# A two-block network on one core: 92 instead of 84 expert chunks computed ahead, a new order of work in the mixers and in the state-space layer

## The chip, the cores and the metric

The kernel runs on one core of one Trainium2 chip. The metric is the device time of one execution in microseconds; before and after are compared by the median of several runs. The core's engines run side by side and each executes its own queue in order: PE (TensorE, matmuls; PEld is its weight load), DVE (VectorE), ACT (ScalarE), POOL (GpSimd) and SP (SyncE, which here only issues DMAs). An engine waits for another through semaphores.

## The reference, cut to what matters

One sequence of 512 tokens of width 1024 goes through two blocks. The first has two linear-attention mixers and a PEER layer (a mixture of 16384 tiny experts); the second has latent attention (MLA), a state-space layer (S5) and two MLPs.

```python
def mixer_output(t, states, n_chunks, hg_norm_g, gla_norm_g, w_br_hg, w_br_gla, w_o):
    o_hg = bidir(t["hg_q"], t["hg_k"], t["hg_v"], t["hg_lg"], states["hg"], n_chunks)       # 8 heads
    o_gla = bidir(t["gla_q"], t["gla_k"], t["gla_v"], t["gla_lg"], states["gla"], n_chunks) # 4 heads
    ...
def peer(h, wq, k1, k2, u, v):
    ...  # per token: 8 heads x top-16 of 16384 experts, and a softmax gate for each
        act = jax.nn.gelu(jnp.einsum("pd,ped->pe", xb, jnp.take(u, eb, axis=0)), approximate=False)
        return jnp.einsum("pe,ped->pd", (gb * act).astype(v.dtype), jnp.take(v, eb, axis=0))
    ...
def s5_mixer(...):
    ...
    _, _, xr, xi = lax.associative_scan(combine, (a_re_t, a_im_t, bu_re, bu_im), axis=1)
    y = (jnp.einsum('blgp,gcp->blgc', xr, c_re) - jnp.einsum('blgp,gcp->blgc', xi, c_im))
    y = y + d_skip * u32
    g = jax.nn.gelu(y)
    z = g * jax.nn.sigmoid(g @ w_glu + b_glu)
    return z @ w_out
```

`bidir` runs a chunkwise decayed attention forward and backward over each head and adds the two.

## The kernel before, in words

The order of each engine's queue comes from a scheduler that simulates the program as written, so the order of the Python calls, the number of buffers of each tile (`bufs`) and the simulated times decide it together. Each fp32 product is computed as three matmul passes over operands split in a high and a low half (`hi x whi`, `lo x whi`, `hi x wlo`); splitting a weight tile of 128 x 1024 costs one ACT cast (`whi`, L387) and one DVE subtraction (`wlo`, L388). A "block" below is one such product of eight 128-row pieces: 24 matmuls.

**Mixers (from 0 to about 1000 us).** First the eight HGRN heads, from about 585 to 856 us the four GLA heads. A GLA head (`gla`) projects values and keys, then the query `ps_q`, then the decays `ps_gk` of both directions (L1043: four short matmuls, whose result goes through ACT and DVE to `lg`), then two gates `ps_g` of 24 matmuls each. `direction` turns one direction's `lg` into a cumulated decay `b` on DVE, transposes the context keys on PE (`pt_c`, L840), multiplies `pkv_c` (L845), computes scores `sc` (L899) and updates states (`pt`, `pkv`).

**PEER (1000 to 2310 us).** 384 of the tokens ("dense", tiles of 384 columns) compute all 16384 experts, 128 at a time, with a matrix of gates that is zero where a token did not choose the expert; the other 128 tokens gather their 128 experts' rows of `u` and `v` by indirect DMA on POOL (`rows`) and multiply on DVE. A chunk `e` of 128 experts has a *hidden* block (`hidden`: weight tile `raw` of `u` from HBM, `pu` on PE, gelu on ACT to `hx` or `kx`), and an output block with the same chunk of `v`. Chunks come in 16 groups of 8. While DVE does the top-k selection (1000 to 1350 us) and then the spread (1350 to 1613 us), PE computes hidden blocks ahead: those of the list `AHEAD` are parked in a DRAM buffer (`he`, 192 KB each) and read back as `hx`; the 16 of `KEPT` (groups 0 and 1) stay in SBUF as `kx`. The spread builds the gate matrix: DVE compares with iota (`o`, L1365 to L1368), PE multiplies (`pg`, L1375), ACT copies (`gs`, L1377), SP writes two halves of a block of 32 tokens to DRAM (`gd`, L1379), 12 blocks. Then in the *weighted phase*, group by group, gates are read back (`gt`, L1095, 12 blocks of 128 columns at once, for 4 chunks), `kx` or `hx` is multiplied with them (L1106), split (`ahi`, `alo`), and eight output blocks (`ps`) add up over the group's chunks. `hx` has `HX` buffers, `gt` has `GT`. A group of which not all hidden chunks were done ahead computes the rest inside the phase: with 84 ahead, two blocks in each of the groups 2 to 15.

**Second block (2310 to 3529 us).** MLA, MLP, then S5 (2935 to about 3160 us), MLP. S5 works in 8 chunks of 128 channels: `project(c)` (`ps_u`, and a round trip of `u` through DRAM), `scan(c)` (`pw` from table `sT`, rotations from `rot` on DVE and POOL), `answer(c)` (`py` from tables `tt` and `cp`), `activate(c)` (a second round trip, gelu, split), then the gate product `ps_g`. The tables were made before and lie in DRAM; `S5In` loads them chunk by chunk, with two buffers for each kind of table.

Of the kernel before, what the change touches and what calls it, by code (L numbers as in the profile page):

```python
# [9 lines left out]
F32 = mybir.dt.float32  # L10
# [20 lines left out]
PI_IN = 3.1415925  # L31


AHEAD = [8 * g + i for i in range(8) for g in range(2, 16)][:84]
KEPT = range(16)

RING = 16
# [7 lines left out]
ADA_DVE = (2,)  # L45
ADA_M = [[2 * j, 2 * j + 1, 8 + 2 * j, 9 + 2 * j] for j in range(4)]
NGLU = 3
S5P = 5
HX = 5
GT = 3  # L50
PIN = True
GPIN = True
# [10 lines left out]
GBLK = TD // GTOK  # L63
# [275 lines left out]

class S5In:  # L340

    SHAPES = (("tt", [8, 128], 2), ("sT", [8, 128], 2), ("cp", [2, 512], 2), ("rot", [2, 2, 256], 2))

    def __init__(self, B, M):
        self.B, self.M, self.got = B, M, {}
# [22 lines left out]
class Build:  # L368
# [613 lines left out]
    def hgrn(self):  # L982
        nc, M, Q, ia = self.nc, self.M, self.Q, self.ia
        for hd in range(NH):
# [3 lines left out]
            keys, lgs = [], []  # L988
# [14 lines left out]
                keys.append(s)  # L1003
                lgs.append(lg)
            q = self.query(ia["w_hg"][hd, 2])
            runs = [self.direction(d, q, keys[d], lgs[d], 1.0, vt, 128, None) for d in range(2)]
            g = self.gate(ia["w_hg"][hd, 3])
            self.outputs(vt, 128, runs, [g], self.col("hgrn_norm_g"), hd)
            if hd == 0:

# [9 lines left out]
    def gla(self):  # L1020
# [7 lines left out]
        for hd in range(NG):  # L1028
# [3 lines left out]
            key = M.tile([128, T + TC], F32, tag="key", bufs=2, name="key")  # L1032
            nc.scalar.copy(out=key[:, 0:T], in_=ps[:])
            nc.scalar.copy(out=key[:, T:T + TC], in_=pc[:])
            q = self.query(ia["w_gq"][hd])
            lgs = []
            for d in range(2):
                bias = self.col("gk_b", d * 4 + hd)
                lg = M.tile([128, T + TC], F32, tag="lg", bufs=2, name="lg")
                parts = []  # L1040
                for t0, n in ((0, T), (T, TC)):
                    ps = self.G.tile([128, n], F32, tag="mm", bufs=3, name="ps_gk")
                    nc.tensor.matmul(ps[:], lhsT=gkw[d * 32:d * 32 + 16, hd * 128:hd * 128 + 128],  # L1043
                                     rhs=gr[d * 32:d * 32 + 16, t0:t0 + n], start=True, stop=True)
                    ex = self.A.tile([128, T], F32, tag="sg", bufs=2, name="ex")
                    nc.scalar.activation(out=ex[:, 0:n], in_=ps[:], func=AF.Abs, bias=bias)
                    parts.append((ex[:, 0:n], lg[:, t0:t0 + n]))
                    nc.vector.tensor_scalar(out=lg[:, t0:t0 + n], in0=ps[:], scalar1=bias, scalar2=0.0, op0=ALU.add,
                                            op1=ALU.min)
                for ex, _ in parts:  # L1050
                    nc.scalar.activation(out=ex, in_=ex, func=AF.Exp, scale=-1.0)
                for ex, to in parts:
                    nc.scalar.activation(out=ex, in_=ex, func=AF.Ln, bias=1.0)
                    nc.vector.tensor_tensor(out=to, in0=to, in1=ex, op=ALU.subtract)
                lgs.append(lg)
            runs = [self.direction(d, q, key, lgs[d], 1.0 / 16.0, vt, 256, None) for d in range(2)]
            gates = [self.gate(ia["w_gg"][2 * hd + i]) for i in range(2)]
            self.outputs(vt, 256, runs, gates, self.col("gla_norm_g", 0, 2), 2 * hd)


# [1 line left out]
    def peer(self):  # L1062
        tc, nc, ia, P = self.tc, self.nc, self.ia, self.P
        with tc.tile_pool(name="peer", bufs=1) as A, tc.tile_pool(name="peerd", bufs=1, space=DRAM) as DR, \
# [23 lines left out]
            with tc.tile_pool(name="pv", bufs=1) as M, tc.tile_pool(name="pvp", bufs=1, space=PSUM) as Q:  # L1088
                gates = {}

                def act(e):
                    g, n = e // 4, 4 * GTOK
                    if g not in gates:
                        gates[g] = M.tile([128, GBLK, n], F32, tag="gt", bufs=GT, name="gt")
                        nc.sync.dma_start(out=gates[g], in_=gd[:].rearrange("b p e t -> p b (e t)")[  # L1095
                            :, :, g * n:(g + 1) * n])
                    gt = gates[g][:, :, (e % 4) * GTOK:(e % 4 + 1) * GTOK]
                    x = kept.get(e)
                    if x is None:
# [722 lines left out]
    def s5_states(self, M, Q):  # L1822
# [89 lines left out]
        scan(0)  # L1912
        done = 0
        for c in range(8):
            if c + S5P < 8:
                project(c + S5P)
            if c < 7:
                scan(c + 1)
            answer(c)
            while done <= c and c + S5P >= 7:  # L1920
                activate(done)
# [43 lines left out]
```

## Time and profile before

| | us |
|---|---|
| runs | 3541.2, 3534.71, 3549.97 (median 3541.2) |
| profiled execution | 3531.33, its span 3529.1, mean granted TensorE clock 0.973 |
| mixers, 0 to 1000 | PE busy 957.53 of 1000 |
| selection and spread, 1000 to 1590 | PE busy 587.68 of 590, 237 GB/s |
| end of spread and weighted phase, 1590 to 2310 | PE busy 688.37 of 720, 308 GB/s |
| second block, 2310 to 3529 | PE busy 1155.39 of 1219, 129 GB/s |

Times in the table are stretches of the profiled execution; busy time is time in which the engine had an instruction running, and the rest is time that it stood idle. PE is idle for 140 us in all, and the clock granted to it is below full in some stretches. So time can come from three places: less work on PE, fewer waits, or a higher clock.

### The profile page before, as it was taken

To read this page: it belongs to the slowest core of one execution; us is meant where nothing else is said; L and a number is where in the kernel's file an instruction comes from. 1 tells how busy PE (TensorE), PEld (TensorE's weight loads), DVE (VectorE), ACT (ScalarE), POOL (GpSimd) and SP (SyncE) were. 2 spreads that over 40 slices of the span, in tenths; PEclk is the share of its full clock that TensorE was granted. 3 is DMA by queue.
4 is the path that set the end of the run, shared out by engine and by line. 5 is a ranking of instruction groups with operands and counts; after the bars stand their busy time and mean duration, and the time that the engine had idled before them with its cause. 6 is when DMAs were issued, how large, how long until landed. Compare 5 with 4: busy or idle time off the path is not lost.

```text
span 3529.1 us, 49456 instructions
## 1 busy us (share of the span) xinstructions
PE 3389.0 (96%) x18457; PEld 2981.8 (84%) x18457; DVE 2496.4 (71%) x4763; ACT 1573.9 (45%) x2480; POOL 620.0 (18%) x459
## 2 busy tenths in 40 slices
PE   8999999999999999996999999999999998899998
PEld 5888878787889999996999999976887778788887
DVE  5566676535657998987988988775897867773335
ACT  5576533545334335774333333344533344343333
POOL 3111100111100312333344444200000002300000
PEclk9999999999999999998999999999999998899999
DMA  5223365112624876889999999611367666523332
GB/s 199 90 84 97 96 209 189 48 37 87 184 72 122 286 243 235 335 298 304 335 319 338 334 339 335 215 57 41 115 209 219 202 188 179 144 79 94 96 96 66
DMA packets 280911, 636.52 MB, mean 180 GB/s; under 512 B 33440, under 2 KB 128800, under 8 KB 277216
## 3 DMA queue, kind: packets, MB, share of 16 engines
q1 hardware_dynamic: 233056, 490.75, 43.1%
q0 software_dynamic: 38144, 138.43, 10.7%
q10 hardware_dynamic: 9472, 4.20, 0.4%
q8 instruction: 145, 2.38, 0.3%
q14 instruction: 94, 0.77, 0.1%
HBM read 573.30 MB, written 64.18 MB: 181 GB/s over the span
## 4 chain that ended last, share of the span: by engine, by line
PE 71%; DVE 14%; DMA 6%; ACT 5%; issue 3%; SPq 1%; POOL 1%; DVEq 0%; ACTq 0%; POOLq 0%
PE ps L400 22%; PE pu L400 11%; PE ps_f L400 6%; PE ps_v L400 4%; PE ps L435 4%; PE ps_q L400 3%; DVE wlo L388 2%; PE pg L1375 2%; PE ps_l L400 2%; DMA modw<-in_modT_dram 2%; PE ps_g L400 2%; DVE modw L542 1%; PE pm L400 1%; PE pb L435 1%; DVE rows L1166 1%
## 5 line engine op out<-in xcount | busy, mean ns | idle before, releaser
L387 ACT CAST whi<-raw 128x1024 fp32r<-128x1024 f32 x547 | 572.1, 1049 | 967.9 <-PE ps L400 274.5
L388 DVE TENSOR_TENSOR wlo<-raw,whi 128x1024 fp32r<-128x1024 f32 x530 | 653.7, 1235 | 309.5 <-ACT whi L387 177.2
L400 PE MATMUL ps<-ahi,whi 128*128 128x384 f32 (+2 forms) x1560 | 330.7, 352 | 24.1 <-ACT ahi L517 19.4
L400 PE MATMUL ps<-alo,whi 128*128 128x384 f32 (+2 forms) x1560 | 334.0, 351 | 1.7 <-DVE alo L518 1.5
L400 PE MATMUL ps<-ahi,wlo 128*128 128x384 f32 (+2 forms) x1560 | 320.8, 347 | 0.0
L400 PEld LDWEIGHTS ps<-ahi,whi 128*128 128x128 f32 x1560 | 275.5, 191 | 50.2 <-ACT ahi L517 24.7
L400 PEld LDWEIGHTS ps<-alo,whi 128*128 128x128 f32 x1560 | 276.2, 189 | 23.0 <-DVE alo L518 3.3
L1145 POOL DMA_INDIRECT rows<-in_u_rows_dram,gidx x128 | 182.7, 1427 | 607.0 <-DVE gact L1166 406.6
L400 PEld LDWEIGHTS ps<-ahi,wlo 128*128 128x128 f32 x1560 | 272.3, 188 | 19.5 <-issue 0.2
L1145 POOL DMA_INDIRECT rows<-in_v_rows_dram,gidx x128 | 204.2, 1595 | 262.5 <-DVE gacc L1181 241.5
L400 PE MATMUL pu<-h_hi,whi 128*128 128x384 f32 x1024 | 203.7, 338 | 1.2 <-ACT hx L1077 1.2
L400 PE MATMUL pu<-h_hi,wlo 128*128 128x384 f32 x1024 | 202.5, 338 | 0.0
L400 PE MATMUL pu<-h_lo,whi 128*128 128x384 f32 x1024 | 201.0, 337 | 0.0
L400 PEld LDWEIGHTS pu<-h_hi,whi 128*128 128x128 f32 x1024 | 178.7, 188 | 2.1 <-ACT hx L1077 2.0
L400 PEld LDWEIGHTS pu<-h_lo,whi 128*128 128x128 f32 x1024 | 179.3, 188 | 0.0
L400 PEld LDWEIGHTS pu<-h_hi,wlo 128*128 128x128 f32 x1024 | 178.7, 188 | 0.1
L1181 DVE SCALAR_TENSOR_TENSOR gacc<-rows,ggate,gacc 128x1024 f32<-128x1024 f32 x127 | 162.4, 1279 | 0.1
L1166 DVE CUSTOM_DVE_ANT_0 rows<-rows,gx 128x1024 f32<-128x1024 f32 x128 | 154.4, 1221 | 2.7 <-DMA rows<-in_u_rows_dram,gidx 2.7
L1400 DVE SCALAR_TENSOR_TENSOR res<-ps,mod,res 128x512 f32<-128x512 f32 (+1 forms) x92 | 62.3, 679 | 113.1 <-PE ps L400 106.5
L388 POOL TENSOR_TENSOR wlo<-raw,whi 128x1024 fp32r<-128x1024 f32 x17 | 43.6, 2584 | 547.8 <-DVE wlo L388 406.2
L400 PE MATMUL ps_f<-h_hi,whi 128*128 128x512 f32 x464 | 119.8, 397 | 1.2 <-ACT whi L387 1.2
L517 ACT CAST ahi<-hx 128x384 fp32r<-128x384 f32 x112 | 56.4, 513 | 143.3 <-DVE hx L1106 143.3
(625 smaller groups left out, 7038.3 us busy)
## 6 DMA issues: line engine op xcount, KB each, us to landing
raw<-in_u_dram SPq DMA_DIRECT2D x128, 512.0 KB, 4.4
raw<-in_v_dram SPq DMA_DIRECT2D x128, 512.0 KB, 5.3
raw<-in_w_dram SPq DMA_DIRECT2D x128, 512.0 KB, 3.6
modw<-in_modT_dram SPq DMA_DIRECT2D x192, 256.0 KB, 4.1
gd<-gs SPq DMA_DIRECT2D x24, 1024.0 KB, 8.0
gt<-gd SPq DMA_DIRECT2D x32, 768.0 KB, 9.9
raw<-in_w_hg_dram SPq DMA_DIRECT2D x32, 512.0 KB, 3.6
res<-in_adaT_dram SPq DMA_DIRECT2D x64, 256.0 KB, 3.5
```

The costliest lines, as they stand in the source:

```text
L387: self.nc.scalar.copy(out=hi[:], in_=raw[:])
L388: (eng or self.nc.vector).tensor_tensor(out=lo[:], in0=raw[:], in1=hi[:].bitcast(F32), op=ALU.subtract)
L400: i = self.nc.tensor.matmul(ps, lhsT=w[a], rhs=x[b], start=start and n == 0, stop=stop and n == last)
L435: self.nc.tensor.matmul(ps[:, tok], lhsT=w[a][:, k], rhs=rhs(k, b, tok), start=(k == 0 and i == 0), stop=(k == 7 and i == 2))
L517: nc.scalar.copy(out=hi, in_=src)
L542: r = nc.vector.tensor_tensor_reduce(out=w[:], in0=w[:], in1=row[i][:], scale=1.0, scalar=start, op0=ALU.mult, op1=ALU.add, accum_out=out[ ...
L1145: self.nc.gpsimd.indirect_dma_start(out=t[:], out_offset=None, in_=self.ia[rows], in_offset=bass.IndirectOffsetOnAxis(ap=self.gidx[:, s:s ...
L1166: i = nc.vector.tensor_tensor_reduce(out=r[:], in0=r[:], in1=x[:], scale=1.0, scalar=0.0, op0=ALU.mult, op1=ALU.add, accum_out=act[:, s:s ...
L1181: i = nc.vector.scalar_tensor_tensor(out=acc[:], in0=r[:], scalar=w, in1=acc[:], op0=ALU.mult, op1=ALU.add)
L1375: nc.tensor.matmul(pg[:, j], lhsT=o2[:, q * 4 + j], rhs=o1[:, q * 4 + j], start=True, stop=True)
L1400: self.nc.vector.scalar_tensor_tensor(out=self.res[:, d, tok], in0=ps, scalar=self.gate1(n)[:, d:d + 1], in1=self.res[:, d, tok], op0=ALU. ...
```

## The change

Five edits. (1) `AHEAD` takes 92 chunks instead of 84: the seventh chunk of the groups 2 to 9 is computed before the weighted phase too. (2) `HX` goes from 5 to 4, and the gates of the first four chunks get a tile of their own in another pool, loaded in three pieces (the blocks 0 to 8, 9 to 10, and 11). (3) An HGRN head's gate is written between its two directions. (4) A GLA head's first decay is written ahead of the query, and gates and directions alternate. (5) In S5 three projections run ahead instead of five, a chunk's project call stands between the scan and the answer, and `tt` and `sT` have three buffers.

```diff
-AHEAD = [8 * g + i for i in range(8) for g in range(2, 16)][:84]
+AHEAD = [8 * g + i for i in range(8) for g in range(2, 16)][:92]
-S5P = 5
-HX = 5
+S5P = 3
+HX = 4
-    SHAPES = (("tt", [8, 128], 2), ("sT", [8, 128], 2), ("cp", [2, 512], 2), ("rot", [2, 2, 256], 2))
+    SHAPES = (("tt", [8, 128], 3), ("sT", [8, 128], 3), ("cp", [2, 512], 2), ("rot", [2, 2, 256], 2))
...
-            runs = [self.direction(d, q, keys[d], lgs[d], 1.0, vt, 128, None) for d in range(2)]
+            runs = [self.direction(0, q, keys[0], lgs[0], 1.0, vt, 128, None)]
             g = self.gate(ia["w_hg"][hd, 3])
+            runs.append(self.direction(1, q, keys[1], lgs[1], 1.0, vt, 128, None))
...
-            q = self.query(ia["w_gq"][hd])
-            lgs = []
-            for d in range(2):
+
+            def decay(d):
...
-                lgs.append(lg)
-            runs = [self.direction(d, q, key, lgs[d], 1.0 / 16.0, vt, 256, None) for d in range(2)]
-            gates = [self.gate(ia["w_gg"][2 * hd + i]) for i in range(2)]
+                return lg
+            lgs = [decay(0)]
+            q = self.query(ia["w_gq"][hd])
+            lgs.append(decay(1))
+            gates = [self.gate(ia["w_gg"][2 * hd])]
+            runs = [self.direction(0, q, key, lgs[0], 1.0 / 16.0, vt, 256, None)]
+            gates.append(self.gate(ia["w_gg"][2 * hd + 1]))
+            runs.append(self.direction(1, q, key, lgs[1], 1.0 / 16.0, vt, 256, None))
...
-                        gates[g] = M.tile([128, GBLK, n], F32, tag="gt", bufs=GT, name="gt")
-                        nc.sync.dma_start(out=gates[g], in_=gd[:].rearrange("b p e t -> p b (e t)")[
-                            :, :, g * n:(g + 1) * n])
+                        cuts = (0, GBLK - 3, GBLK - 1, GBLK) if g == 0 else (0, GBLK)
+                        gates[g] = (A if g == 0 else M).tile([128, GBLK, n], F32, tag=f"gt{min(g, 1)}",
+                                                             bufs=GT if g else 1, name="gt")
+                        for b0, b1 in zip(cuts, cuts[1:]):
+                            nc.sync.dma_start(out=gates[g][:, b0:b1], in_=gd[b0:b1].rearrange("b p e t -> p b (e t)")[
+                                :, :, g * n:(g + 1) * n])
...
         for c in range(8):
+            if c < 7:
+                scan(c + 1)
+
             if c + S5P < 8:
                 project(c + S5P)
-            if c < 7:
-                scan(c + 1)
             answer(c)
```

In the HGRN heads no engine's queue changes: the first row of PE that differs stands in the first GLA head. The three places below show what the scheduler makes of the rest. In each row stand the line, the operation, output and input tiles, the shape, and how often the row repeats; "before" is the first fence of each place.

**Place 1: PE at the third GLA head**, from the last projection to the first transposes. Before, the four `ps_gk` stand together behind `ps_q`:

```order
L400 MATMUL ps_q<-h_hi,whi 128x512 x8
L400 MATMUL ps_q<-h_lo,whi 128x512 x8
L400 MATMUL ps_q<-h_hi,wlo 128x512 x8
L1043 MATMUL ps_gk<-gr,gkw 128x512
L1043 MATMUL ps_gk<-gr,gkw 128x256
L1043 MATMUL ps_gk<-gr,gkw 128x512
L1043 MATMUL ps_gk<-gr,gkw 128x256
L400 MATMUL ps_g<-h_hi,whi 128x512 x8
L400 MATMUL ps_g<-h_lo,whi 128x512 x8
L400 MATMUL ps_g<-h_hi,wlo 128x512 x8
L400 MATMUL ps_g<-h_hi,whi 128x512 x5
L840 MATMUL pt_c<-ident,ck 128x128 x2
```

After, at the same place of the same engine:

```order
L1043 MATMUL ps_gk<-gr,gkw 128x512
L1043 MATMUL ps_gk<-gr,gkw 128x256
L400 MATMUL ps_q<-h_hi,whi 128x512 x8
L400 MATMUL ps_q<-h_lo,whi 128x512 x8
L400 MATMUL ps_q<-h_hi,wlo 128x512 x8
L1043 MATMUL ps_gk<-gr,gkw 128x512
L1043 MATMUL ps_gk<-gr,gkw 128x256
L400 MATMUL ps_g<-h_hi,whi 128x512 x8
L400 MATMUL ps_g<-h_lo,whi 128x512 x8
L400 MATMUL ps_g<-h_hi,wlo 128x512 x8
L840 MATMUL pt_c<-ident,ck 128x128 x2
```

The first two `ps_gk` moved ahead of the 24 `ps_q`, and the second gate moved behind the first direction's transposes, scores and states (not shown). In the first head `pt_c` stands directly behind the second pair of `ps_gk`, ahead of both gates.

**Place 2: SP at the end of the spread** (`gd` are the spread's writes, `gt` the gates read back, `raw` weight tiles of `u` and `v`). Before:

```order
L1379 DMA gd<-gs 128x2048 x2
L378 DMA raw<-in_v_dram 128x1024 x4
L1379 DMA gd<-gs 128x2048 x2
L378 DMA raw<-in_v_dram 128x1024 x2
L1379 DMA gd<-gs 128x2048 x4
L1095 DMA gt<-gd 128x12x128 x8
L378 DMA raw<-in_v_dram 128x1024 x8
```

After, the same engine from the ninth block's writes on:

```order
L1390 DMA gd<-gs 128x2048 x2
L1106 DMA gt<-gd 128x9x128
L378 DMA raw<-in_u_dram 128x1024 x4
L1390 DMA gd<-gs 128x2048 x2
L378 DMA raw<-in_u_dram 128x1024 x3
L1390 DMA gd<-gs 128x2048 x2
L378 DMA raw<-in_u_dram 128x1024
L1106 DMA gt<-gd 128x2x128
L378 DMA raw<-in_v_dram 128x1024 x3
L1390 DMA gd<-gs 128x2048 x2
L1106 DMA gt<-gd 128x128
L378 DMA raw<-in_v_dram 128x1024
```

Two of the three pieces of the first gates now stand ahead of the last write, three loads of `v` stand directly ahead of it, and eight loads of `u` came in. On PE the last six `pg` rows, which stood alone before, now have five hidden blocks (`pu`) between them, and three more blocks stand between the last `pg` and the first `ps`.

**Place 3: SP around the start of S5** (`tt`, `sT`, `rot`, `cp` are the tables of a chunk, `w_su` and `w_glu` weights, `decay` the last load ahead of the layer). Before:

```order
L378 DMA raw<-in_w_dram 128x1024 x2
L378 DMA raw<-in_w_su_dram 128x1024 x6
L1848 DMA decay<-d_dec 64x2x32 x2
L378 DMA raw<-in_w_su_dram 128x1024 x2
L378 DMA raw<-in_w_glu_dram 128x1024 x3
L359 DMA sT<-d_s 128x1024
L378 DMA raw<-in_w_glu_dram 128x1024
L359 DMA sT<-d_s 128x1024
```

After, from the same two weight loads on:

```order
L378 DMA raw<-in_w_dram 128x1024 x2
L378 DMA raw<-in_w_su_dram 128x1024
L359 DMA tt<-d_t 128x1024
L359 DMA sT<-d_s 128x1024
L378 DMA raw<-in_w_su_dram 128x1024 x5
L1859 DMA decay<-d_dec 64x2x32 x2
L378 DMA raw<-in_w_su_dram 128x1024 x2
L378 DMA raw<-in_w_glu_dram 128x1024 x3
L359 DMA sT<-d_s 128x1024 x2
```

The two big tables of the third chunk, 512 KB each, moved from behind the `w_glu` loads to ahead of `decay`; where one `sT` stood behind the first `w_glu` loads, two now stand together.

## Rows read from the trace of the kernel before

**Rows 1.** The page: the chain that ended last, shares by engine.

```profile
PE 71%; DVE 14%; DMA 6%; ACT 5%; issue 3%; SPq 1%; POOL 1%; DVEq 0%; ACTq 0%; POOLq 0%
```

**Rows 2.** Windows: length; busy PE, PEld, DVE, ACT, POOL; PE clock, DMA share, GB/s.

```profile
602.00:856.00 254.00, 241.46 (x1352) 198.09 (x1351) 118.85 (x228) 138.36 (x204) 30.54 (x32) 0.94 0.15 46
...
1590.00:1655.00 65.00, 37.48 (x191) 32.46 (x190) 44.01 (x70) 24.22 (x58) 16.91 (x13) 0.76 0.89 288
1660.00:1700.00 40.00, 39.74 (x225) 38.44 (x224) 39.38 (x63) 16.43 (x24) 18.94 (x15) 1.00 0.90 318
1708.00:2214.00 506.00, 503.34 (x2877) 501.10 (x2876) 447.87 (x568) 183.64 (x241) 216.01 (x138) 1.00 0.95 335
2900.00:2940.00 40.00, 32.79 (x238) 31.56 (x238) 33.37 (x90) 21.83 (x47) 1.95 (x4) 0.91 0.04 13
2940.00:3030.00 90.00, 81.52 (x464) 73.40 (x463) 63.99 (x70) 22.58 (x28) 27.10 (x32) 0.85 1.00 261
```

**Rows 3.** Timeline, 1588 to 1660: start, length, instruction, idle before and releaser.

```profile
1590.21 0.59 PE L400 MATMUL pu<-h_hi,wlo 128*128 128x384 f32 x2
...
1611.52 1.16 PE L1375 MATMUL pg<-o,o 128*128 128x128 f32 x8 [0.95 <-ACT gs L1377]
...
1625.35 0.56 DVE L1106 TENSOR_TENSOR kx<-gt,kx 128x384 f32<-128x384 f32 x1 [16.06 <-DMA gt<-gd]
...
1626.50 1.33 PE L400 MATMUL ps<-ahi,whi 128*128 128x384 f32 x3 [13.83 <-ACT ahi L517]
...
1652.18 1.62 PE L400 MATMUL ps<-ahi,whi 128*128 128x384 f32 x8 [2.03 <-DVE res L1139]
```

**Rows 4.** The chain that ended last, 1590 to 1660: start, length, what.

```profile
1613.69 5.99 DMA gd<-gs
1619.83 5.39 DMA gt<-gd
```

**Rows 5.** PE's timeline in the weighted phase, 1700 to 1800.

```profile
1707.79 1.56 PE L400 MATMUL pu<-h_hi,whi 128*128 128x384 f32 x8
...
1711.96 1.55 PE L400 MATMUL pu<-h_hi,whi 128*128 128x384 f32 x8
...
1749.65 1.56 PE L400 MATMUL pu<-h_hi,whi 128*128 128x384 f32 x8
```

**Rows 6.** A window of 10 us inside the weighted phase.

```profile
1970.00:1980.00 10.00, 10.00 (x59) 10.00 (x58) 8.33 (x14) 4.51 (x7) 3.26 (x2) 1.00 1.03 389
```

**Rows 7.** DMA issues, 1655 to 2255: KB each, median us from issue to landing.

```profile
DMA packets 93024, 196.49 MB, mean 327 GB/s; under 512 B 6573, under 2 KB 53557, under 8 KB 92981
...
hx<-he SPq DMA_DIRECT2D x79, 192.0 KB, 7.0
```

**Rows 8.** DMA in the first 60 us: GB/s in 40 slices, and a small load.

```profile
GB/s 0 96 148 305 418 421 494 426 393 426 415 399 410 407 412 412 407 407 410 410 415 407 412 381 385 389 410 251 36 330 307 48 5 287 57 0 0 0 0 0
...
ident<-in_ident_dram SPq DMA_DIRECT2D x1, 64.0 KB, 3.0
```

**Rows 9.** PE's waits in the GLA heads, 602 to 834: us in total, times, longest.

```profile
PE pkv_c L845 <- ACT ktc L842: 3.8, 2, 2.9
PE ps_gk L1043 <- DVE lg L1048: 3.2, 4, 1.4
...
PE ps_gk L1043 <- ACT q L979: 1.4, 1, 1.4
```

**Rows 10.** PE's timeline at the last GLA head, 800 to 835.

```profile
815.98 3.78 PE L400 MATMUL ps_g<-h_hi,whi 128*128 128x512 f32 x8
...
822.38 2.03 PE L400 MATMUL ps_g<-h_hi,wlo 128*128 128x512 f32 x8
```

**Rows 11.** PE's waits in S5, 2940 to 3065.

```profile
PE ps_g L435 <- ACT h_hi L517: 6.1, 1, 6.1
PE pw L1855 <- DMA sT<-d_s: 4.9, 1, 4.9
PE py L1890 <- ACT yo L1895: 2.6, 1, 2.6
```

## The prediction

> **What bounds the kernel now.** I read the chain of the page first: PE holds 71% of what ends last, DVE 14%, DMA 6% [rows 1]. Then I cut the span by stage [rows 2]. PE is busy 503.34 of 506 us in the weighted phase, so what leaves PE there leaves the time, as long as DVE (447.87) and DMA (share 0.95, 335 GB/s) keep up. Three stretches hold idle time or a lowered clock: the end of the spread (PE busy 37.48 of 65, clock 0.76), the GLA heads (241.46 of 254, clock 0.94) and the start of S5 (81.52 of 90, clock 0.85, DMA share 1.00, while the 40 us before it move 13 GB/s). The timeline, the chain and the waits then say who is late in each [rows 3, 4, 9, 11]. The sum is made against the profiled execution, 3531.33 us (span 3529.1 and 2.2 around it). It lies 9.9 below the median of the runs, so I add the change to both: the predicted time is the median plus the sum.
>
> **HGRN: 0.** No queue changes, so this edit can't move anything.
>
> **Eight more chunks ahead: the gain.** One hidden block takes 1711.96 - 1707.79 = 4.17 us of PE [rows 5]. The groups 2 to 9 lose one each: 8 x 4.17 = -33.4 us.
>
> **What they cost at the end of the spread: +10.** The last hidden block ends at 1590.8, the last `pg` at 1612.7 [rows 3]. The six `pg` rows between are 96 recorded matmuls, twelve times the eight of the row at 1611.52; at about 1.0 us each (1.16 with its pipelined end) that is 12 us of work in 21.9, so 10 idle. Five blocks (20.9 us) go in there, which is 11 more than fit: last `pg` at 1590.8 + 12 + 20.9 = 1623.7, +11. From there the chain was `gs`, then `gd` 5.99 us, then `gt` 5.39, then DVE at 1625.35 [rows 3, 4]. The last piece of the gates is now 64 KB instead of 768; the nearest row, a 64 KB load, takes 3.0 us [rows 8], so -2.4. The last write now stands behind three `v` loads on SP, each of which may have to wait for a weight buffer; the queue behind it is the 64 KB piece and with it everything in group 0. I take +1 (below 0 if buffers are free, above 4.17 if one must wait for a block to be used). First product on DVE: 1625.35 + 11 - 2.4 + 1 = 1635. The three blocks behind the last `pg` keep PE busy until 1623.7 + 12.5 = 1636.2, so the 13.83 us that PE stood before group 0 [rows 3] are filled, and group 0 starts at 1636.5 instead of 1626.5: +10. Bounds +7 (`pg` at 0.9, SP free) and +14 (a blocked `v` load).
>
> **Group 0 itself: -3.** Its later gates came late (the 2.03 us wait at 1652.18 [rows 3]) and PE ran after a long idle stretch. Now the second gate tile is loaded early and PE comes from 20 us of dense work. I take the 2.0 and 1 for the clock; bounds 0 and -6.
>
> **Can DVE and DMA follow in groups 2 to 9? +9.** A group takes 41.86 us [rows 5] and would take 37.69. DVE: 447.87/506 x 41.86 = 37.05 us a group, less one weight split; it fits, and DVE and PE were seen at 39.38 and 39.74 of 40 together [rows 2]. DMA: 335 GB/s x 41.86 = 14.02 MB a group; one `u` tile of 512 KB becomes one `hx` read of 192 KB, 13.69 MB, so 363 GB/s are asked for. If share 1.00 is the ceiling of this mix, that is 335/0.95 = 353 GB/s, or 38.8 us: 1.1 late, 8.9 in eight groups. One 10 us window shows 389 GB/s [rows 6], the first 60 us some 410 [rows 8]: bound below, 0. Bound above: 335 is all that row gathers and gate reads allow: 13.69/0.335 = 40.9, 3.2 x 8 = +25.6. I take 9.
>
> The Trainium skill has a rule that speaks against this edit: "DMA: Bandwidth & Descriptors", section Specifications, gives a core about 358 GB/s of HBM. By it a group would last 38.2 us and the slip would be 4.4, the time 3507. The 389 and 410 GB/s of the rows lie above that figure, so the trace does not show it as a ceiling for this core; the term above goes by the share.
>
> **GLA: -7.** Before, the second pair of `ps_gk` waits for buffers that DVE frees through `lg`, and the first for ACT: 3.2 + 1.4 us in the waits; another 3.8 is `pkv_c` waiting for the transposed keys [rows 9]. After these short matmuls the gate runs slow: its first eight take 3.78 us and the second eight still more than the 2.03 of the third [rows 10]. In this head the excess is 1.75 in the first eight alone; with about 1 in the second, four heads make some 11, an estimate. With 24 `ps_q` matmuls (three times 2.03) between the pairs, the `lg` and `ps_q` waits should go (-4.6), and about half of the slow clock (-5.4). Against it: in the first head `pt_c` follows the second pair without a gate between as cover; DVE and ACT need longer than PE's work in front, and I take the longest wait of that kind, 2.9 [rows 9]. Sum -7.1; bounds -19 (all waits and all of the excess) and +4 (nothing gained, and that stall).
>
> **S5: -5.** The DMA engines are full from 2940 to 3030 and idle before. The third chunk's `tt` and `sT` (1.05 MB) now go out before 2940; at 261 GB/s [rows 2] that frees 4.0 us, and the wait for `sT` (4.9) is the place where it would show [rows 11]. Fewer projections ahead remove none: they only let scans start earlier. The last activations may start later, since `activate` now begins with chunk 4. I take -5; bounds -13.6 (all three waits of [rows 11]) and +4 (a later round trip through DRAM, no transfer saved).
>
> **Sum.** -33.4 + 10 - 3 + 9 - 7.1 - 5 = -29.5: 3501.8 for the profiled execution, **3512** on the median's scale.
>
> **Rivals.**
> (a) *DMA becomes the bound in the groups 2 to 9.* For it: share 0.95 already, and a mean of 327 GB/s over the whole phase, in which nothing moved faster for long [rows 7]. Against: the windows above 363. It gives +25.6 instead of +9: 3528, no change that can be told.
> (b) *GLA and S5 give nothing*: the clock falls after any pair of short matmuls, and S5's DMA stays full with the other chunks' tables. For it: share 1.00 over 90 us, of which 4 us of transfers leave. It gives -17.4: 3524, on the line.
> (c) *Slower: `hx` with four buffers.* The groups 2 to 9 now read seven `hx` instead of six, with four buffers instead of five, so the second four can only be asked for when the first are split. A read lands after 7.0 us [rows 7]. If the eight chunks are taken in one burst at the border of a group, with one hidden block less as cover, PE waits up to 7.0 x 8 = 56: 3568. It decides from 5.9 us a border on ((29.5 + 17.7)/8). Against it: PE lost only 2.7 us in twelve borders before [rows 2].
> That the HGRN edit does nothing is certain and in the sum.
>
> **How the numbers follow.** About 0.5% (18 us) is what a measurement of this kernel tells from no change, so faster means below 3523.5. Forecast 0.58 (its own range 3495 to 3523, faster); (a) 0.17, no change; (b) 0.17, about half below the line; (c) 0.08, nearly all slower. Faster 0.58 + 0.09 = 0.67, no change 0.17 + 0.08 + 0.01 = 0.26, slower 0.07. For the range: all good ends together would give -65 (3476) and all bad ones +14 (3555); neither is likely, so I cut to 3483 and, to hold (a) and (b), 3540.
>
> **What would show it.** Right: five `pu` blocks among the last `pg`, first `kx` product near 1635 plus what the earlier stages moved, no idle PE before the first `ps`; one `pu` block in each of eight group borders and 38 to 39 us a group there, 42 in the rest; no `lg` wait at `ps_gk`, first eight `ps_g` near 2 us; no 4.9 wait for `sT`. Wrong: groups of 40 us or more with DMA share 1.00 (a); the same slow `ps_g` and a wait of about 5 for a table in S5 (b); PE or DVE waiting for `hx` at each border, or SP held at a `v` load while `gs` is ready (c). It would also fail if the phase's DVE work, which is not reduced but moved by eight splits, came to bind: then groups stay near 41 with DVE full.

## The result, and the profile after

The changed kernel takes 3504.57 us (median of 4 runs, 3500.86 to 3511.98) against 3540.62 before (4 runs): ratio 0.9897, 95% interval 0.988 to 0.9914, so 36 us faster. The two profiled executions, 3531.33 and 3504.06, differ by 27 only. The profiled execution of before was a lucky one: 27 later runs of that kernel lie between 3531.36 and 3557.09, with a median of 3543.55, so all of them are slower than it.

To place the gain I use the first and last start of a tile's matmuls in the view of that tile, here of the kernel after (count, shortest/median/longest ns, first to last start):

```profile
L400 PE MATMUL pm<-h_hi,whi x128: 392/396/802, 443.7 to 919.3; 128*128 128x512 f32 x128
L937 PE MATMUL o<-qd,st x256: 271/275/583, 116.2 to 847.3; 128*128 128x128 f32 x128
L400 PE MATMUL pu<-h_hi,whi x1024: 332/336/446, 1086.7 to 2240.7; 128*128 128x384 f32 x171
L400 PE MATMUL ps_u<-h_hi,whi x40: 389/396/503, 2916.7 to 2964.6; 128*128 128x512 f32 x40
L400 PE MATMUL ps_g<-h_hi,wlo x40: 395/396/396, 3039.4 to 3063.4; 128*128 128x512 f32 x40
```

The same lines of the kernel before (`ps_g` over the whole kernel, so with a larger count and an earlier first start):

```profile
L400 PE MATMUL pm<-h_hi,whi x128: 387/396/794, 442.7 to 927.8; 128*128 128x512 f32 x128
L937 PE MATMUL o<-qd,st x256: 271/275/582, 115.9 to 855.7; 128*128 128x128 f32 x128
L400 PE MATMUL pu<-h_hi,whi x1024: 332/336/445, 1095.1 to 2263.4; 128*128 128x384 f32 x171
L400 PE MATMUL ps_u<-h_hi,whi x40: 389/395/504, 2939.5 to 2972.6; 128*128 128x512 f32 x40
L400 PE MATMUL ps_g<-h_hi,wlo x168: 392/395/479, 98.8 to 3090.5; 128*128 128x512 f32 x168
```

Three intervals come out of them: **G**, from the first `pm` (the first mixer's merge) to the last `o` (the last GLA head), 847.3 - 443.7 = 403.6; **P**, from there to the last hidden block, 2240.7 - 847.3 = 1393.4; **S**, from the first `ps_u` to the last `ps_g`, 3063.4 - 2916.7 = 146.7. Before they were 413.0, 1407.7 and 151.0. Between P and S both kernels take 676.

The windows of [rows 2], moved along with their stages, with the weighted phase cut in two behind the groups 2 to 9 (length; busy PE, PEld, DVE, ACT, POOL; PE clock, DMA share, GB/s):

```profile
598.00:848.00 250.00, 242.10 (x1375) 200.99 (x1374) 120.36 (x229) 129.16 (x201) 29.18 (x34) 0.97 0.16 49
1590.00:1655.00 65.00, 58.85 (x318) 55.11 (x317) 46.26 (x69) 30.12 (x59) 15.82 (x11) 0.87 0.91 304
...
1705.00:2022.00 317.00, 307.50 (x1747) 304.08 (x1746) 288.15 (x381) 109.96 (x146) 130.91 (x92) 1.00 0.98 348
2028.00:2195.00 167.00, 166.62 (x955) 166.30 (x955) 149.57 (x183) 60.22 (x79) 69.81 (x47) 1.00 0.96 339
...
2917.00:3007.00 90.00, 82.60 (x505) 73.38 (x505) 68.61 (x76) 25.24 (x32) 28.28 (x33) 0.92 0.93 257
```

The GLA heads run at a granted clock of 0.97 instead of 0.94. At the end of the spread PE is busy for 58.9 of 65 us; before it was 37.5. The price stands in the window from 1705 to 2022: in the groups 2 to 9, PE now idles 9.5 us of 317 with the DMA engines at 0.98, while it idles 0.4 of 167 in the groups behind them, which still compute two blocks each.

PE's timeline where [rows 3] showed the gap of 13.83 us before group 0:

```profile
1612.43 1.95 PE L1386 MATMUL pg<-o,o 128*128 128x128 f32 x16
...
1625.32 1.55 PE L400 MATMUL pu<-h_hi,wlo 128*128 128x384 f32 x8
1626.71 0.69 PE L400 MATMUL ps<-ahi,whi 128*128 128x384 f32 x3
```

The first `ps` follows the last `pu` without idle time. SP's queue beside it:

```profile
1613.93 0.33 SPq L378 DMA_DIRECT2D raw<-in_v_dram  x1
1615.02 0.80 SPq L1390 DMA_DIRECT2D gd<-gs  x2
1619.93 0.32 SPq L1106 DMA_DIRECT2D gt<-gd  x1
```

The loads of `v` do not hold up the last write, which goes out as soon as `gs` is copied; 4.9 us later the last 64 KB of gates are asked for, and DVE's first product starts at 1624.05, 9.0 us after the write was issued. Before it was 12.0 ([rows 3, 4], 1625.35 - 1613.33).

Only a part of these 3.0 us comes from the smaller read. A block of gates goes out in two writes, the chunks 0 to 63 and then 64 to 127. These are the times from issue to landing of the last two, after and before (with two writes, the least and the most are the two themselves):

```profile
DMA to landing us min/median/max: 4.9/6.7/8.4
```

```profile
DMA to landing us min/median/max: 3.9/5.0/6.0
```

Of the two, the tile of the first four chunks needs the first alone. The last piece leaves 0.01 us after that one has landed (0.02 in e1 below, which has the pieces too). The whole tile leaves only behind the second write, in before and in e4, 0.15 and 0.13 us after it has landed. From the read's issue to the first product it is 4.1 us after and 5.5 before, so the smaller read gives 1.4; the other 1.6 come from leaving behind the first write. Why the whole tile waits for the second write, of which it reads nothing either, is not shown.

PE at the last GLA head, as in [rows 10]:

```profile
805.73 1.55 PE L1043 MATMUL ps_gk<-gr,gkw 16*128 16x512 f32 x4
807.39 2.14 PE L400 MATMUL ps_g<-h_hi,whi 128*128 128x512 f32 x8
```

Four records of `ps_gk` without a wait between, and the first eight `ps_g` in 2.14 us instead of 3.78. But in the same head the query, which now stands behind the first pair of `ps_gk`, starts slowly, at a granted clock of 0.53 (1.2 instead of 2.4 GHz for nearly all of it):

```profile
798.48 3.58 PE L400 MATMUL ps_q<-h_hi,whi 128*128 128x512 f32 x8 [1.12 <-ACT key L1035]
```

So in this head the slow stretch moved and did not go. PE's waits in the GLA heads, for [rows 9], and in S5, for [rows 11]:

```profile
PE ps_q L400 <- ACT key L1035: 2.4, 2, 1.2
PE pt_c L840 <- DVE ck L836: 1.8, 1, 1.8
```

```profile
PE ps_g L435 <- ACT h_hi L517: 8.8, 2, 8.0
PE py L1901 <- ACT yo L1906: 4.2, 2, 3.5
```

The waits of `ps_gk` for `lg` and for `q`, and those of `pkv_c` for `ktc`, are gone; these two smaller ones and one of `ps_g` for `q` (0.8) came in their place. In S5 the wait for `sT` is gone, and those for the last activation and for `yo` grew by 2.7 and 1.6.

### The profile page after: what moved, and what is told of

Read it like the earlier page. It is cut to its first block, busy times and chain, and to the rows that moved or that the text cites. A ratio compares the mean times of both kernels' runs of the same rounds, so it can differ in the third digit from the quotient of the medians.

```text
span 3502.2 us, 49513 instructions
## 1 busy us (share of the span) xinstructions
PE 3375.6 (96%) x18457; PEld 2971.0 (85%) x18457; DVE 2493.7 (71%) x4763; ACT 1560.8 (45%) x2473; POOL 599.7 (17%) x459
## 4 chain that ended last, share of the span: by engine, by line
PE 69%; DVE 15%; DMA 8%; issue 4%; ACT 3%; SPq 1%; POOL 1%; ACTq 0%; DVEq 0%; POOLq 0%
PE ps L400 18%; PE pu L400 11%; PE ps_f L400 7%; PE ps_v L400 4%; PE ps L435 4%; PE ps_q L400 3%; PE ps_g L400 3%; DVE wlo L388 3%; PE pg L1386 2%; PE ps_l L400 2%; DMA modw<-in_modT_dram 2%; DMA hx<-he 2%; DVE rows L1177 1%; DVE modw L542 1%; PE pm L400 1%
## 5 line engine op out<-in xcount | busy, mean ns | idle before, releaser
L1156 POOL DMA_INDIRECT rows<-in_v_rows_dram,gidx x128 | 185.0, 1446 | 261.9 <-DVE gacc L1192 235.0
L517 ACT CAST ahi<-hx 128x384 fp32r<-128x384 f32 x112 | 56.0, 512 | 156.0 <-DVE hx L1117 155.9
```

What stands on the lines that cost most here:

```text
L517: nc.scalar.copy(out=hi, in_=src)
L1156: self.nc.gpsimd.indirect_dma_start(out=t[:], out_offset=None, in_=self.ia[rows], in_offset=bass.IndirectOffsetOnAxis(ap=self.gidx[:, s:s ...
```

## The experiments

All ratios are to the kernel before, run beside each kernel on the same chip (27 runs of it for e1 to e4, 13 for e5 to e8, 10 for e9 to e12; medians 3543.55, 3544.7 and 3543.05). G, P and S come from one profiled execution of each kernel, as above.

| kernel | median us, ratio (95%) | G | P | S |
|---|---|---|---|---|
| before | 3540.62 | 413.0 | 1407.7 | 151.0 |
| after | 3504.57, 0.9897 (0.988 to 0.9914) | 403.6 | 1393.4 | 146.7 |
| e1 PEER edits only | 3532.26, 0.9966 (0.995 to 0.9982) | 418.2 | 1394.6 | 156.0 |
| e2 GLA order only | 3525.07, 0.9947 (0.9923 to 0.9971) | 401.7 | 1413.8 | 153.0 |
| e3 S5 edits only | 3540.8, 0.9978 (0.9961 to 0.9996) | 421.3 | 1412.6 | 146.8 |
| e4 92 chunks alone | 3539.97, 0.9996 (0.9979 to 1.0013) | 417.9 | 1406.0 | 152.5 |
| e5 extra chunks spread out | 3510.35, 0.992 (0.9895 to 0.9945) | 401.7 | 1393.7 | 147.0 |
| e6 one gather of `v` rows | 3499.88 (one run) | 404.2 | 1391.2 | 146.3 |
| e7 short sum on DVE | 3502.62 (one run) | 400.8 | 1397.3 | 144.3 |
| e8 GLA decay only | 3527.11, 0.9959 (0.9942 to 0.9976) | 405.8 | 1407.7 | 149.7 |
| e9 gates in one piece | 3524.71, 0.9947 (0.9928 to 0.9966) | 404.2 | 1400.5 | 149.3 |
| e10 98 chunks | 3507.3, 0.9907 (0.9883 to 0.9932) | 401.4 | 1399.3 | 147.4 |
| e11 88 chunks | 3514.08, 0.9927 (0.9902 to 0.9951) | 401.3 | 1397.0 | 146.8 |
| e12 third S5 buffers only | 3532.18 (one run) | 412.7 | 1412.0 | 143.2 |

### e1, e2, e3: one part each on the kernel before

```diff
 e1:
-AHEAD = ...[:84]
+AHEAD = ...[:92]
-HX = 5
+HX = 4
+                        cuts = (0, GBLK - 3, GBLK - 1, GBLK) if g == 0 else (0, GBLK)   # and the loads by pieces
 e2:
+            lgs = [decay(0)]
             q = self.query(ia["w_gq"][hd])
+            lgs.append(decay(1))        # and gate 0, direction 0, gate 1, direction 1
 e3:
-S5P = 5
+S5P = 3                                 # third tt, sT; scan, project, answer
```

> The kernel before with only the PEER edits: 92 chunks ahead, four hx buffers, the first gates in three pieces. My theory: the eight blocks fill the idle PE at the spread's end and the groups 2 to 9 lose one block each, of which the DMA gives back some 14 us; 17 us faster than before (ratio 0.995), and first matmul of group 0 8 to 9 us later than before. Rival 'interaction': the PEER edits pay only because the mixers hand over earlier; then under 8 us faster (0.998 or more).

> The kernel before with only the GLA order (first decay ahead of the query, gates and directions alternating). My theory: 8 to 9 us faster (ratio 0.9975), all of it before 860 us: the waits of ps_gk for lg and for ACT gone, the clock over the GLA heads at 0.97 instead of 0.94, and the same distance carried to the end since the PEER layer starts earlier by as much. Rival 'swallowed': the PEER layer's start is set by a transfer or by DVE, and the end moves by 3 us or less.

> The kernel before with only the S5 edits (three projections ahead, project between scan and answer, third buffers for tt and sT). My theory: 2 to 5 us faster, the 4.9 us wait for sT gone, the wait of ps_g for the last activation still there. Rival 'no gain': the tables of the later chunks keep the DMA engines full and the sT wait comes back as another wait: within 1 us of before.

By the ratios e1 is 12 us faster, e2 19, e3 8 (the medians of e3 and before lie only 3 apart, and its interval reaches from 1 to 14); the three ratios multiply to 0.9891, and the change has 0.9897. So the parts add within their intervals, and "interaction" and "swallowed" fall. The theories for e1 and e3 hold, with e1 at the low end in time (12 instead of 17) and on the mark in P. e2 misses its number: it brings twice what was expected. The intervals say why. G is 402.4 on average in the eight kernels with the new order (400.8 to 404.2), and 416.6 in the five with the old one (412.7 to 421.3): 14.2 us. The other 5 of e2's 19 lie within its interval (10 to 27). The profiled execution of before stands with 413.0 near the low end. In e3's profile, which has the old order, the second head reads:

```profile
678.22 1.54 PE L1043 MATMUL ps_gk<-gr,gkw 16*128 16x512 f32 x2 [1.36 <-ACT q L979]
680.52 1.22 PE L1043 MATMUL ps_gk<-gr,gkw 16*128 16x256 f32 x2 [0.76 <-DVE lg L1048]
681.67 3.78 PE L400 MATMUL ps_g<-h_hi,whi 128*128 128x512 f32 x8
```

The same eight matmuls of this head took 3.78 us in e1 and e4 too; in the third head they took 3.78, 3.66, 2.13 and 3.38 in before, e1, e3 and e4. So the old order's cost is partly a matter of the execution.

### e8: the first decay alone

```diff
+            lgs = [decay(0)]
             q = self.query(ia["w_gq"][hd])
+            lgs.append(decay(1))
             runs = [self.direction(d, q, key, lgs[d], 1.0 / 16.0, vt, 256, None) for d in range(2)]
             gates = [self.gate(ia["w_gg"][2 * hd + i]) for i in range(2)]
```

> The kernel before with only the first decay ahead of the query in the GLA heads; gates and directions in the order of before. Theory 'clock': the four short ps_gk matmuls in a row with waits between them make PE idle enough that the gate behind them runs at the low clock; split by 24 dense matmuls, the first eight ps_g take 2.0 to 2.2 us instead of 2.1 to 3.8, so most of the GLA edit's 15 us (from the merge's start to the last o: 402 to 407 us instead of 413 to 421). Rival 'order of gates': the second gate as cover for the first direction's chain carries it; then this one gains 5 us or less (412 or more).

G is 405.8, inside the expected range: the decay ahead of the query carries about 11 of the 14 us (in time 15 of e2's 19), against "order of gates". But the expected sign is missing. The gate behind the second pair still runs slow in three of four heads:

```profile
742.98 3.66 PE L400 MATMUL ps_g<-h_hi,whi 128*128 128x512 f32 x8 [0.86 <-ACT q L979]
746.43 2.08 PE L400 MATMUL ps_g<-h_lo,whi 128*128 128x512 f32 x8
...
810.10 2.71 PE L400 MATMUL ps_g<-h_hi,whi 128*128 128x512 f32 x8 [0.86 <-ACT q L979]
```

So "clock" is wrong as stated: splitting the four short matmuls does not by itself keep this gate fast. The waits for `lg`, `q` and `ktc` (8.4 us in [rows 9]) went from their places, but others of 6.2 us came: `ps_q` for the keys and `ps_g` for `q` 2.2 each, `pt_c` 1.8. PE over G in before, e8 and after (length, busy; clock, DMA share, GB/s):

```profile
442.68:855.74 413.06, 392.55 (x2101) 0.94 0.34 112
```

```profile
442.79:848.64 405.85, 387.57 (x2101) 0.96 0.34 114
```

```profile
443.69:847.30 403.61, 387.53 (x2102) 0.96 0.35 115
```

The same matmuls keep PE busy for 387.6 us in e8 instead of 392.6, and it idles 18.3 instead of 20.5. As means over the kernels with the old and the new order, PE idles 22.7 and 16.1 us and is busy 393.9 and 386.3: about half of the 14.2 us are waits and the other half is a higher clock, though not at the gate where I looked for it. Where exactly the clock was lost in the old order, and how much the gates' order adds, stays open: 3 us between one profile of e8 and the mean of the new order is within what G varies.

### e4 and e9: what the three pieces are worth

```diff
 e4: the kernel before with
-AHEAD = ...[:84]
+AHEAD = ...[:92]
 e9: the changed kernel with
-                        cuts = (0, GBLK - 3, GBLK - 1, GBLK) if g == 0 else (0, GBLK)
+                        gates[g] = M.tile([128, GBLK, n], F32, tag="gt", bufs=GT, name="gt")   # one load
```

> The kernel before with 92 chunks ahead and nothing else: hx keeps five buffers, the first gates one tile read whole. My theory: the saved blocks are the gain, so 12 to 17 us faster; without the pieces the first product on DVE waits for the whole gate tile (5.4 us instead of 3) and group 0 starts 2 to 3 us later than with the PEER edits together. Rival 'pieces': the three pieces carry the gain, since without them the gates land 10 us later, PE stands again before group 0 and only 5 us or less are left. Rival 'buffers': four hx buffers cost, so this one is faster than the PEER edits together by 3 us or more and its groups 2 to 9 take 38.5 us instead of 39.8.

> The changed kernel with the first gates as one tile read whole, as before (hx keeps four buffers, 92 chunks ahead). Theory 'pieces': the whole tile can only be asked for behind the last write of the spread, so the first product on DVE comes some 10 us after that write's copy instead of 3 to 4, PE stands before group 0 again and the time is 8 to 12 us longer than the changed kernel's (about 3514, ratio 0.9925). Rival 'buffers': the loss of the kernel with 92 chunks alone came from its hx and gate buffers, so here, with four hx, the time is within 3 us of the changed kernel's.

Eight more chunks ahead and nothing else bring nothing that can be told (0.9996). My expectation for e4 is refuted and "pieces" holds. PE's first `ps` in e4 and in e9:

```profile
1649.13 0.79 PE L400 MATMUL ps<-ahi,whi 128*128 128x384 f32 x3 [3.70 <-ACT ahi L517]
```

```profile
1631.01 1.33 PE L400 MATMUL ps<-ahi,whi 128*128 128x384 f32 x3 [3.86 <-ACT ahi L517]
```

PE stands 3.7 us in e4 and 3.9 in e9. The chain of e9 has the second half of the last write with 8.63 us and the whole tile with 5.24 between `gs` and DVE, and the first product comes 14.5 us after `gs` is copied, against 9.0 after the change; I had expected 10 against 3 to 4. P is 7 us longer in e9 than after, and 11 longer in e4 than in e1. Of that, 4.7 and 6.6 stand ahead of the first `ps`, counted from the last `o`. The rest lies in the groups behind: in e4 PE waits 10.6 us for the weight split in the groups 2 to 9 (3.8 in e1). e9's time is 18 us above the changed kernel's by the ratios, more than P explains: 15 us stand between P and S (690.7 us; 672 to 683 in all other kernels), behind the code that this edit touches. There PE is busy 10 us longer, at a granted clock of 0.96 instead of 0.98, and idles 5 more. Why stays open. "Buffers" is refuted as far as `hx` goes: four `hx` with one piece are slow. The pieces came together with a tile of their own for the first gates, so one gate buffer more, and both kernels without the pieces lack that too. No kernel with the own tile and one load was tried, so what this buffer does in the groups behind is not told apart.

### e5, e6, e7: why the groups 2 to 9 are late

After the change the first hidden blocks of group 2's and group 10's border start at

```profile
1704.68 1.56 PE L400 MATMUL pu<-h_hi,whi 128*128 128x384 f32 x8
1706.08 1.57 PE L400 MATMUL ps<-ahi,whi 128*128 128x384 f32 x8
...
1710.29 1.56 PE L400 MATMUL pu<-h_lo,whi 128*128 128x384 f32 x8
...
2022.97 1.56 PE L400 MATMUL pu<-h_hi,whi 128*128 128x384 f32 x8
```

so from mark to mark it is 318.3 us, 39.8 a group. Before, the marks of the same eight lay 337.5 apart, from 1707.79 [rows 5] to

```profile
2045.26 1.56 PE L400 MATMUL pu<-h_hi,whi 128*128 128x384 f32 x8
```

and less 33.4 that is 304.1. But the first mark moved: after the change the last output block of group 1 (4.2 us, from 1706.08 to 1710.29) stands inside group 2's hidden block, and before it stood ahead of it. Without it the eight groups take 314.1 us, 39.3 each, and give 10 us back, not 14. PE's idle time says much the same: 9.9 us from 1690 to 2060, 1.9 before.

```diff
 e5: -AHEAD = [8 * g + i for i in range(8) for g in range(2, 16)][:92]
     +AHEAD = [...][:84] + [8 * g + 6 for g in (2, 4, 6, 8, 10, 12, 14, 15)]
 e6: -            r = self.gather("v_rows", s)
     +            if s == 0:
     +                r = self.gather("v_rows", s)
 e7: -  scalar_tensor_tensor(out=acc[:], in0=r[:], scalar=w, in1=acc[:], ...)
     +  scalar_tensor_tensor(out=acc[:, 0:128], in0=r[:, 0:128], scalar=w, in1=acc[:, 0:128], ...)
```

> The changed kernel, but the eight extra chunks ahead are the seventh of the groups 2, 4, 6, 8, 10, 12, 14 and 15 instead of 2 to 9. Same work, same bytes in the phase. Theory 'DMA': the groups 2 to 9 take 39.8 us instead of 37.7 because weights of v land late when every group asks for 363 GB/s; spread over the phase, 348 GB/s are asked for on average and the queue of weight buffers carries the difference: the phase is 8 to 14 us shorter than in the changed kernel (first to last hidden block 522 to 528 instead of 536). Rival 'DVE' (DVE at 91% is what makes the groups late) and rival 'buffers' (seven hx through four buffers) : every group with one block is late by 2 us wherever it stands, so no gain, 536.

> The changed kernel with one gather of rows of v instead of 128 (all 128 steps on DVE use the first tile, so the gathered tokens' output is not the reference's); DVE does the same work, some 66 MB less move in the phase. Theory 'DMA': the groups 2 to 9 fall from 39.8 to 37.7 or 38 us and the waits of ACT's weight split for v go from 77 us to a small rest. Rivals 'DVE' and 'buffers': still 39.5 or more.

> The changed kernel with the sum over gathered rows of v taken on 128 of 1024 columns (the gathered tokens' output is not the reference's); all transfers stay, DVE is relieved of about 1 us in each of 127 steps. Theory 'DMA': groups 2 to 9 stay at 39.5 us or more. Rival 'DVE': they fall to 38.

The window from 1750 to 2010 of after, e6 and e7, in this order:

```profile
1750.00:2010.00 260.00, 250.87 (x1424) 247.77 (x1423) 235.35 (x303) 89.18 (x119) 106.52 (x76) 1.00 0.98 349
```

```profile
1750.00:2010.00 260.00, 257.02 (x1459) 255.59 (x1458) 241.38 (x315) 93.31 (x124) 9.94 (x7) 0.99 0.69 220
```

```profile
1750.00:2010.00 260.00, 251.25 (x1422) 249.14 (x1421) 181.18 (x305) 88.02 (x118) 96.93 (x78) 0.99 0.97 349
```

Without the gathers of `v` rows PE is busy 257 instead of 251 us, though DVE has as much to do; the last five of the eight groups take 37.7 us each (1831.66 to 2020.34), the full saving. Until about 1795 gathers of `u` rows still run there, with the DMA engines at 0.96 and then 0.85, and the groups are still late. P is only 2 us shorter in this one profile, in which group 0 also starts 3.6 us later. With DVE relieved from 235 to 181 us nothing moves: 40.1 us a group from mark to mark. So transfers make the groups late and DVE does not; and as e6 still has four `hx`, "buffers" falls too. The wait through which it reaches PE is that of ACT's weight split, in the same window, after and e6:

```profile
ACT whi L387 <- DMA raw<-in_v_dram: 59.4, 24, 5.4
```

```profile
ACT whi L387 <- DMA raw<-in_v_dram: 25.5, 10, 6.5
```

e5 refutes the other half of that theory. Spread over all groups, the eight blocks lead to the same P, 1393.7 instead of 1393.4. But what the rivals expected, that each group with one block is late by 2 us wherever it stands, does not hold either. The borders of the groups 4 and 5, and of 12 and 13, in e5:

```profile
1789.80 1.56 PE L400 MATMUL pu<-h_hi,whi 128*128 128x384 f32 x8
...
1827.68 1.56 PE L400 MATMUL pu<-h_hi,whi 128*128 128x384 f32 x8
...
2112.08 1.56 PE L400 MATMUL pu<-h_hi,whi 128*128 128x384 f32 x8
...
2157.45 1.56 PE L400 MATMUL pu<-h_hi,whi 128*128 128x384 f32 x8
```

The groups 4, 6, 8 and 10, with one block each, take 37.7 to 38.8 us; group 12 takes 45.4, and PE's longest wait in it is 3.2 us for the weight split. So the loss does not fall on each of them. In e5 the DMA engines are at share 0.96 and 343 GB/s from 1690 to 2060, against 0.98 and 348 where the one-block groups stand together, so there was little room to shift load into; that this is why spreading gained nothing is argued, not shown. Of the three edits only fewer bytes shortened the eight groups as a whole: 311.8 us from mark to mark in e6 instead of 318.3.

### e10, e11: how many blocks

```diff
 e10: -[:92]  +[:98]        e11: -[:92]  +[:88]
```

> The changed kernel with 98 chunks ahead: the seventh chunk of all groups 2 to 15. Theory 'idle time is used up': PE has no idle time left at the spread's end, so the six blocks cost there what they save later (25 us each way), and six more groups ask for 363 GB/s and are 1.8 us late each: 8 to 14 us slower than the changed kernel (ratio 0.992 to 0.994). Rival 'fewer blocks in the phase are always a gain': 5 us or more faster than the changed kernel (ratio 0.988 or less).

> The changed kernel with 88 chunks ahead: four blocks fewer are moved. Theory: four blocks (16.7 us) fit into the idle time that the spread's end had (about 23 us) and only four groups are late by 1.8 us, so it gains 16.7 - 7 = 10 us against 84, as the 92 do: within 4 us of the changed kernel. Rival 'every block counts': half of the PEER gain, 6 to 9 us slower than the changed kernel.

P is 5.9 longer with 98 than with 92, and 3.6 longer with 88. In time, 98 is 0.9907, not to be told from 0.9897: the expected loss of 8 to 14 us is not seen, and the rival's gain is not either. For 88, P fits the theory and the time (0.9927) the rival; the intervals overlap, so this does not decide. What e10 shows is that six more blocks bring nothing that can be told; whether 88 are worse than 92 stays open.

### e12: the third buffers alone

```diff
-    SHAPES = (("tt", [8, 128], 2), ("sT", [8, 128], 2), ...
+    SHAPES = (("tt", [8, 128], 3), ("sT", [8, 128], 3), ...
```

> The kernel before with only the third buffers for tt and sT in S5 (five projections ahead, project ahead of scan as before). Theory 'early table': the third chunk's tables go out before the layer and the wait of 4.9 us for sT goes, so from the first ps_u to the last ps_g it takes 146 to 149 us instead of 150 to 156. Rival 'order': the order of project, scan and answer carries the gain, and this kernel stays at 150 or more.

S is 143.2, the shortest of all; the old order with two buffers has 149.7 to 156.0 (mean of five 152.4), the full S5 edit 146.8 on average over eight kernels. So the early tables carry the gain and "order" falls, as far as one profile shows it. PE's waits in e12:

```profile
PE py L1890 <- ACT yo L1895: 5.5, 2, 3.4
PE ps_g L435 <- DVE h_lo L518: 4.4, 2, 2.4
PE ps_g L435 <- ACT h_hi L517: 4.4, 3, 2.2
```

The longest wait of `ps_g` for an activation is 2.4 here and 8.0 after the change, so the new order may cost some 3 us; one profile does not settle it, and a kernel with the change and the old S5 order was not tried.

## Why the prediction was right, point by point

It said 3512 (3483 to 3540) and 3504.57 came. The sum by stage, with measured values as differences of the means over kernels with and without the edit: PEER -17.4 forecast and -16.8 measured (P 1410.8 in the five kernels with 84 chunks; 1394.0 in after and e1), S5 -5 and -5.6, GLA -7.1 and -14.2. The measured three make -36.6, the time -36. In the two profiled executions alone they are -14.3, -4.3 and -9.4, in all -28, close to the -29.5 that was worked out from one of them.

- **HGRN 0**: right; the queues are the same.
- **The gain of -33.4**: right as a count of blocks.
- **Spread's end, +10**: seen from the last `o`, group 0 starts 8.6 us later (779.4 instead of 770.8). The steps hold: PE is the bound, and SP was not held up (forecast +1). That the last piece shortens the chain is right (3.0 us, forecast 2.4), but the size is luck: I counted the smaller read alone, which gave 1.4, and did not see that the piece would wait for one write instead of two, which gave 1.6. With blocks on PE beside it the second write lands 8.4 to 8.6 us after its issue (6.0 before), so one read of the whole tile is dearer there: in e4 and e9, without the pieces and their own tile, 7 to 11 us go.
- **Group 0, -3**: wrong, and small. From the first `ps` to the first `pu` it took 81.3 us and takes 78.0, but that is the output block that moved behind the mark: with its 4.2 us it is 82.2, +0.9. The 2.0 us wait is gone as said; the other waits behind the first `ps` grew from 4.1 to 6.0.
- **DMA in the groups 2 to 9, +9**: measured +10, near the chosen value and far from rival (a) with 25.6. The estimate by the share, 353 GB/s, is nearly what the window shows: 348 to 349 at 0.98. At 349 the 13.69 MB take 39.2 us; 39.3 were measured. The Trainium skill's figure in "DMA: Bandwidth & Descriptors", Specifications, some 358 GB/s for a core, would have given 4.4 us; this mix stops below it, although [rows 6] and [rows 8] lie above it.
- **GLA, -7**: the mis-sized term, too small by half. The step that failed is its basis: waits and slow matmuls were counted in one execution, which was among the fastest that this kernel has, and then half of the clock was taken. The other old-order profiles show up to 8 us more in G. The sub-step that `ps_gk` split by `ps_q` cures the clock at the gate is not borne out either (e8; in the last head after the change `ps_q` itself is slow). In the means 6.6 us of the 14.2 are idle time and 7.6 are busy time at a lower clock; the forecast had 4.6 of waits and 5.4 of clock, less 2.9 for a new stall. The feared stall of `pt_c` in the first head is there and smaller, 1.8 instead of 2.9.
- **S5, -5**: right in size and place; the `sT` wait is gone. What I gave no price of its own, the later activations, shows as the longer wait for `h_hi`.
- **Rivals**: (a) is there in part, with the DMA engines at 0.98 but 10 us instead of 25.6; (b) wrong for both stages; (c) not seen: DVE waits for `hx` are 10.5 us from 1690 to 2060, 12.6 before.
- **The basis of 9.9 us**: the gap was a rightful warning that the profile was not a typical run. Adding the change to the median assumed that a typical run gains as much as this fast one. It gains more: the two profiles differ by 27, the medians by 36, and G stood at 413.0 in the fast run against 416.6 in the mean. So the forecast of 3512 is 7 us too high, about what the GLA term missed.

## What to carry to other kernels

Moving work from a full stage into an idle stretch pays only if what waits behind that stretch still comes in time: the blocks alone gained nothing here, and with the gate tile read in three pieces they paid. A piece can also free a read from a write that it does not need. Before costing a stage at a lowered clock, look whether the runs of the kernel spread: one profile may stand at either end. When a busier stage leaves, its neighbour shows: at a DMA share of 0.95 there were 14 GB/s left, and moving load within the phase did not help, taking bytes away did.

## What the runs showed of the hardware

- The same instructions in the same order took 2.13 to 3.78 us for eight matmuls (third GLA head: 3.78, 3.66, 2.13, 3.38 in four profiles); over the 3.78 the granted clock is 0.50, over the 2.13 it is 1.00. The kernel before spread over 26 us in 27 runs. The changed kernel's four stay within 11, but four runs of before stay within 15, so a smaller spread is not shown. The granted clock of a whole run went with its time: 0.981 at 3500.86 and 3505.08, 0.979 at 3504.06, 0.976 at 3511.98.
- This mix of weight tiles, row gathers and gate reads stopped at 349 GB/s with the DMA engines at 0.98 (DVE full) and 0.97 (DVE relieved).
- Two writes of 1 MB to DRAM issued 0.4 us apart at the end of the spread landed 4.9 and 8.4 us after their issue after the change, 5.2 and 8.6 in e1, 5.3 and 8.6 in e4, and 3.9 and 6.0 in before, where SP issued no weight load beside them. A read of 64 KB behind the first took 4.1 us after, one of 768 KB behind the second 5.4 in before and 5.2 in e9.
